# A decoder layer on one NeuronCore: pair b reordered and partly premade, three pairs by seven products in the first down linear, eight block sums made every seven chunks

## The chip, the cores and the metric

The kernel runs on one core of one Trainium2 chip. The metric is the device time of one execution in microseconds (us). Five engines work side by side, each with its own instruction stream in a fixed order: TensorE (PE in the profile, its weight loads PEld), VectorE (DVE), ScalarE (ACT), GpSimd (POOL) and SyncE (SP). SP and POOL issue the transfers (DMAs) between main memory (HBM) and on-chip memory (SBUF). TensorE writes its sums into eight PSUM banks.

## The reference, cut to what matters

One hybrid decoder layer in float32 on 272 tokens (16 learned meta tokens and 256 real ones), width 2048, feed-forward width 5632:

```python
h = rms_norm(s, norm_ffn1);  s = s + 0.5 * swiglu_ffn(h, ffn1_w_gu, ffn1_w_down)
h = rms_norm(s, norm_mix)
q, k, v, b_gate, c_gate, u = split(h @ w_in)
y_att  = diff_attention(q, k, v, lam, subln)          # 8 heads, causal, a = p0 - lam * p1
y_conv = b_gate * short_conv(c_gate * u, conv_w)      # 3 taps
gates = sigmoid(h @ w_gate)                           # two branches
merged = gates0 * (y_att @ w_branch0) + gates1 * (y_conv @ w_branch1)
s = s + merged @ w_out
h = rms_norm(s, norm_ffn2);  s = s + 0.5 * swiglu_ffn(h, ffn2_w_gu, ffn2_w_down)
return rms_norm(s, norm_final)[:, 16:]
```

Nearly all of the time is in the matrix products with the large weights.

## The kernel before, in words

**Float32 by three products.** Every float32 operand is split in two parts, high and low: weights into tiles `wh` (a cast on ScalarE) and `wl` (the rest, a subtraction on VectorE), activations likewise. A product is three matmuls: high by `wh`, low by `wh`, high by `wl`. So each weight tile costs TensorE its matmuls, ScalarE one cast and VectorE one subtraction; a tile of 128x1024 weights is loaded by SP into a buffer `st` (three buffers), and `wh` and `wl` have four buffers each.

**Stages.** In order: the first feed-forward (lines `pg`, `pu`, `pd`), then `k` (first half), `q`, `b`, `v` (first half), `k`, `v` (second halves), `c`, `u`, `c`, `u`, then four times gates `g` and branch product `z`, then `w_out`, then the second feed-forward in three parts, each of some gate-and-up units followed by two down linears (`pd`), one for each half of the output columns ("long" down linears in the first two parts, 16 chunks each).

**Seven products instead of eight.** The functions `linear` and `linear_tok` do plain products. `linear_mix` treats its input in pairs of chunks as a 2x2 by 2x2 block product. A plan gives a kind to each pair: "D" does the eight block products (24 matmuls of 128x512), "S" and "P" do seven products (21 matmuls) on sums of weight blocks and sums of activation blocks. For S the sums of the weight blocks (tiles `t13` and `t24`) are made by VectorE in place, three additions over 128x2048 elements in all; for P they were made earlier in the program, stored to HBM in a tensor `made`, and are loaded by two SP transfers of 512 KB beside a shorter weight load. A plan has four parts: the kinds by position, the positions after which transposes that have been put off (`later`) are done, where the sums of a later S are made, and the order of the pairs (empty: 0 to 7). `t13` and `t24` come from a pool `tt` of two buffers. In a D pair four PSUM banks are in use; once an S or P pair has begun, all eight are, until the products end.

**Making the sums ahead.** An object of class `Making` makes half of one pair's sums: `fetch` loads four weight blocks (512 KB, tile `mk`) by a POOL transfer, `add` does three VectorE additions, `store` writes the result (512 KB) by a POOL transfer. Steps are hung on `tick`, which `linear` calls once per chunk of the plain linears. Ticks 0 to 511 are the first feed-forward and make 54 pairs, with three fetches ahead. Ticks 528 to 639 are the seven linears from `v` to `u` (16 ticks each). There `tick_later` makes the pairs in `MADE_LATER`, one after the other: at a step it emits the add and the store of the last fetched half and then the next fetch, into one of the two `tt` buffers in turn. POOL issues these in order, so a fetch goes out behind the store before it, and a store behind its add. An add stands in VectorE's stream and waits there for its fetch; whatever VectorE has behind it waits too.

**What stands around the attention.** From the second `k` on, work of the attention is put between chunks: `scores` of one unit (matmuls `sc_ps`, then on VectorE lines 960 to 975 with exponentials on ScalarE between), and in the next step `turn` (TensorE transposes `aT`, which read `sc`) and `values`. The order of each engine's instructions is fixed at build time by a scheduler that merges these streams.

## Time and profile before

| | |
|---|---|
| median of 3 runs | 2124.77 us (2124.61 to 2125.13) |
| the profiled execution's own time | 2126.45 us |
| its span, first to last instruction | 2124.7 us |
| TensorE matmul busy | 2112.8 us, 13087 matmuls |
| VectorE busy | 1780.5 us |
| ScalarE busy | 1151.1 us |
| granted TensorE clock | 0.999 |
| stretch of b | 856.6 to 900.0 us |
| stretch of v to u | 900.0 to 1092.5 us |
| first gates unit g | 1092.5 to 1133.3 us |
| first long down linear, first half of the columns | 1600.8 to 1643.2 us |

The profile is of one execution, whose own time is 1.68 us above the median. Times inside it are counted from its first instruction. A row of the timeline gives start, duration, engine, line, operation, what is written and read, and in brackets the engine's idle time before it and what ended that. Line numbers are those of the kernel before; in the changed kernel they are one to three higher in the parts spoken of.

### The profile page before, as it was taken

The numbers are of one execution on the slowest core, as the hardware profiler recorded it, in microseconds if no ns is written. First come the engines' busy times: TensorE is split into PE (matmuls) and PEld (weight loads), VectorE is DVE, ScalarE is ACT, GpSimd is POOL, SyncE is SP. The second block draws the span as 40 slices with busy tenths as digits, with TensorE's granted clock in tenths as the row PEclk, the third lists the DMA queues.
The fourth block names the chain that finished last, engine by engine and source line by source line (L and its number), as shares of the span: only waits on it lengthen the run. The fifth ranks groups of instructions, "written<-read, shape, count | busy, mean of one in ns | idle before, by whom it ended". The sixth has DMA issues, their size and how long they took to land. (4 is left out here: it accounts for less than half of the span.)

```text
span 2124.7 us, 33643 instructions
## 1 busy us (share of the span) xinstructions
PE 2112.8 (99%) x13087; PEld 1910.3 (90%) x13087; DVE 1780.5 (84%) x2490; ACT 1151.1 (54%) x1453; POOL 164.6 (8%) x261
## 2 busy tenths in 40 slices
PE   9999999999999999999999999999999999999998
PEld 9999999999999998899998888887888888888887
DVE  8777776677777778978888899999999899998998
ACT  6434443344443445655456565567775567656765
POOL 0111111111121110000000000000000100000000
PEclk9999999999999999999999999999999999999999
DMA  7989999999889785565565665567885988779963
GB/s 303 338 316 331 344 338 327 334 325 335 332 326 340 296 301 196 202 227 199 209 220 201 233 213 190 201 225 242 314 298 194 287 316 302 261 228 314 325 236 139
DMA packets 111328, 576.47 MB, mean 271 GB/s; under 512 B 12992, under 2 KB 13376, under 8 KB 71104
## 3 DMA queue, kind: packets, MB, share of 16 engines
q1 hardware_dynamic: 74160, 444.66, 58.4%
q0 software_dynamic: 36576, 128.99, 17.4%
q8 instruction: 102, 1.67, 0.3%
q10 hardware_dynamic: 432, 0.67, 0.1%
q14 instruction: 58, 0.48, 0.1%
HBM read 506.11 MB, written 63.96 MB: 268 GB/s over the span
## 5 line engine op out<-in xcount | busy, mean ns | idle before, releaser
L429 ACT CAST wh<-st 128x1024 fp32r<-128x1024 f32 x320 | 335.2, 1049 | 471.3 <-PE pu L446 145.7
L434 DVE TENSOR_TENSOR wl<-st,wh 128x1024 fp32r<-128x1024 f32 x320 | 390.5, 1223 | 211.4 <-ACT wh L429 211.2
L552 DVE TENSOR_TENSOR wl<-st,wh 128x1024 fp32r<-128x1024 f32 (+1 forms) x424 | 453.5, 1085 | 44.4 <-ACT wh L551 40.1
L551 ACT CAST wh<-st 128x1024 fp32r<-128x1024 f32 (+1 forms) x424 | 386.6, 942 | 172.4 <-PE pdx L665 43.2
L551 ACT CAST wh<-t 128x1024 fp32r<-128x1024 f32 x214 | 224.6, 1053 | 201.9 <-DVE t L707 83.9
L552 DVE TENSOR_TENSOR wl<-t,wh 128x1024 fp32r<-128x1024 f32 x214 | 257.9, 1221 | 29.9 <-ACT wh L551 26.0
L447 PE MATMUL pd<-mh,wl 128*128 128x272 f32 x704 | 203.1, 288 | 0.0
L445 PE MATMUL pg<-h,wh 128*128 128x272 f32 x704 | 201.8, 287 | 1.0 <-ACT wh L429 1.0
L445 PE MATMUL pd<-mh,wh 128*128 128x272 f32 x704 | 202.2, 287 | 0.0
L445 PE MATMUL pu<-h,wh 128*128 128x272 f32 x704 | 201.9, 287 | 0.0
L447 PE MATMUL pu<-h,wl 128*128 128x272 f32 x704 | 201.7, 287 | 0.0
L446 PE MATMUL pu<-h,wh 128*128 128x272 f32 x704 | 201.7, 287 | 0.0
L446 PE MATMUL pg<-h,wh 128*128 128x272 f32 x704 | 201.6, 287 | 0.0
L447 PE MATMUL pg<-h,wl 128*128 128x272 f32 x704 | 201.1, 287 | 0.1
L446 PE MATMUL pd<-ml,wh 128*128 128x272 f32 x704 | 200.8, 285 | 0.0
L664 PE MATMUL pg<-wh,h 128*128 128x512 f32 x375 | 146.4, 390 | 0.3 <-ACT wh L551 0.3
L665 PE MATMUL pg<-wh,h 128*128 128x512 f32 x375 | 146.7, 391 | 0.0
L666 PE MATMUL pg<-wl,h 128*128 128x512 f32 x375 | 146.0, 389 | 0.0
L339 POOL DMA_DIRECT2D made<-mk x118 | 86.1, 729 | 760.0 <-DVE mk L333 608.4
L445 PEld LDWEIGHTS pg<-h,wh 128*128 128x128 f32 x704 | 132.6, 188 | 1.2 <-ACT wh L429 1.2
L446 PEld LDWEIGHTS pd<-ml,wh 128*128 128x128 f32 x704 | 133.5, 190 | 0.0
L447 PEld LDWEIGHTS pg<-h,wl 128*128 128x128 f32 x704 | 132.1, 188 | 0.6 <-DVE wl L434 0.5
(392 smaller groups left out, 5100.7 us busy)
## 6 DMA issues: line engine op xcount, KB each, us to landing
st<-in_ffn_w_gu_dram SPq DMA_DIRECT2D x118, 1024.0 KB, 7.5
st<-in_ffn_w_down_dram SPq DMA_DIRECT2D x82, 1024.0 KB, 7.3
mk<-in_ffn_made_of_dram POOLq DMA_DIRECT2D x118, 512.0 KB, 8.5
made<-mk POOLq DMA_DIRECT2D x118, 512.0 KB, 6.6
t<-made SPq DMA_DIRECT2D x118, 512.0 KB, 5.9
st<-in_ffn_w_gu_dram SPq DMA_DIRECT2D x54, 768.0 KB, 6.0
st<-in_w_in_dram SPq DMA_DIRECT2D x32, 1024.0 KB, 5.4
st<-in_w_gate_dram SPq DMA_DIRECT2D x27, 1024.0 KB, 4.8
```

What stands on the lines that cost most here:

```text
L339: last_store[:] = [nc.gpsimd.dma_start(out=self.unit[self.p][:, :, cs], in_=self.t).ins]
L429: nc.scalar.copy(out=wh[:, :m, :], in_=sw)
L434: last_wl[:] = [nc.vector.tensor_sub(wl[:, :m, :], sw, wh[:, :m, :].bitcast(F32)).ins]
L445: nc.tensor.matmul(a, wh[:, i, f], act.part(c, 0, t0, t1), start=first, stop=False)
L446: nc.tensor.matmul(a, wh[:, i, f], act.part(c, 1, t0, t1), start=False, stop=False)
L447: nc.tensor.matmul(a, wl[:, i, f], act.part(c, 0, t0, t1), start=False, stop=last)
L551: part_last[:] = [nc.scalar.copy(out=wh, in_=src).ins]
L552: part_last.append(nc.vector.tensor_sub(wl, src, wh.bitcast(F32)).ins)
L664: nc.tensor.matmul(ps[k], hi, wh, start=first, stop=False)
L665: nc.tensor.matmul(ps[k], lo, wh, start=False, stop=False)
L666: nc.tensor.matmul(ps[k], hi, wl, start=False, stop=left[k] == 0)
```

## The change

The diff, cut to its core:

```diff
-B_PLAN = ("DSDSDSDS", (2, 4), {(0, 1): 1, (2, 1): 3, (4, 1): 5, (6, 1): 7}, ())
+B_PLAN = ("DDSDSDPS", (1, 1), {(1, 1): 2, (3, 1): 4, (6, 3): 7}, (0, 2, 1, 4, 3, 6, 7, 5))
...
+DOWN_MADE = ("DDDPDSDP", (1,), {(4, 1): 5}, (0, 1, 3, 4, 5, 6, 7, 2))
...
-MADE = [(0, d, p) for d, plan in enumerate(GATE_UNITS) for p, kind in enumerate(plan[0]) if kind == "P"]
+MADE = [(3, 1, 7)]
+MADE += [(0, d, p) for d, plan in enumerate(GATE_UNITS) for p, kind in enumerate(plan[0]) if kind == "P"]
...
-MADE_LATER = [(0, 0, 1), (0, 0, 3), (1, 1, 5), (1, 2, 1), (1, 3, 1)]
+MADE_LATER = [(0, 0, 1), (0, 0, 3), (1, 1, 5), (1, 2, 1), (1, 3, 1), (2, 0, 4), (2, 0, 2), MADE[-1]]
...
-LATER_TICKS = (TICK_COUNT + 16, TICK_COUNT + 124)
+LATER_TICKS = [TICK_COUNT + 16 + 7 * i for i in range(2 * len(MADE_LATER))] + [TICK_COUNT + 127]
...
     def tick_later(n):
-        n0, n1 = LATER_TICKS
-        steps = len(spare_later) + 1
-        i = (n - n0) * steps // (n1 - n0)
-        if not n0 <= n < n1 or (n > n0 and i == (n - 1 - n0) * steps // (n1 - n0)):
+        if n not in LATER_TICKS:
             return
+        i = LATER_TICKS.index(n)
...
-            if p in turn_at and later:
-                later.pop(0)()
+            for _ in range(turn_at.count(p)):
+                if later:
+                    later.pop(0)()
...
-            mixed(B_PLAN, hm, w_qb[1], "b", b_end)
+            mixed(B_PLAN, hm, w_qb[1], "b", b_end, made[3][1], True)
...
-                side.extend([lambda: None] * 2)
-                side.extend(lambda p=p: ma.sum_of_parts(p) for p in (4, 6))
-                side.extend((lambda: None, lambda ma=ma: ma.sum_of_parts(2)))
-                add_mix(DOWN_FIRST, ma, w_down, half[0] * GC, u, 0.5, "dma", lambda: None)
+                for p in (None, 4, None, 6, 2) if half is thirds[0] else (None, None, 4, 6, None, 2):
+                    side.append((lambda: None) if p is None else lambda ma=ma, p=p: ma.sum_of_parts(p))
+                if half is thirds[0]:
+                    add_mix(DOWN_MADE, ma, w_down, 0, u, 0.5, "dma", lambda: None, made[2][u])
+                else:
+                    add_mix(DOWN_FIRST, ma, w_down, half[0] * GC, u, 0.5, "dma", lambda: None)
```

In b the pairs 1, 3, 5 and 7 are done by seven products, as before, but two D pairs come first, pair 7 is of kind P with sums made in the first feed-forward, and all four put-off transposes of q come after position 1. In the first long down linear (first half of the columns) pairs 4, 6 and 2 are done by seven products, 4 and 2 of them premade; before, pairs 4 and 6 were. `MADE_LATER` has eight pairs, 16 halves, with a step every seven ticks from tick 528 and a last one at tick 639, the last chunk of u; before it had five pairs, ten halves, at 11 steps over 108 ticks.

Three places show how the instructions move. First, TensorE in b. `qb_ps` are the put-off transposes of q (from `cgate` and `cup`), `bx` and the other `b_` are b's eight products, `h_` and `sp_` the activations. Before, near the end of b:

```order
L664 MATMUL b_9799<-wh,h_123 128x512
L889 MATMUL qb_ps<-ident,cgate 128x128 x8
L665 MATMUL b_9799<-wh,h_123 128x512
L889 MATMUL qb_ps<-ident,cup 128x128 x8
L666 MATMUL b_9799<-wl,h_123 128x512
```

In the changed kernel, inside the second D pair (those from `cup` stand in the same way twelve matmuls later, behind it):

```order
L664 MATMUL bx<-wh,h_118 128x512
L665 MATMUL bx<-wh,h_118 128x512
L666 MATMUL bx<-wl,h_118 128x512
L890 MATMUL qb_ps<-ident,cgate 128x128 x8
L664 MATMUL b_9795<-wh,h_118 128x512
L665 MATMUL b_9795<-wh,h_118 128x512
L666 MATMUL b_9795<-wl,h_118 128x512
```

The transposes have moved from the last pair of b, where they stand between the three matmuls of one product, to the ends of two D tiles early in b.

Second, VectorE in the attention, in the first u linear, at the softmax of one unit (`rs`, `sc` and `scM`). Before, this stands there:

```order
L434 TENSOR_TENSOR wl<-st,wh 128x1024
L971 RECIPROCAL rs<-sm 128x2
L972 TENSOR_TENSOR rs<-rs,lam 128x1
L973 TENSOR_SCALAR sc<-sc,rs 128x272
L975 SCALAR_TENSOR_TENSOR sc<-sc,rs 128x256
L975 SCALAR_TENSOR_TENSOR scM_9120<-sc,rs 128x16
```

Now:

```order
L434 TENSOR_TENSOR wl<-st,wh 128x1024
L972 RECIPROCAL rs<-sm 128x2
L973 TENSOR_TENSOR rs<-rs,lam 128x1
L333 TENSOR_TENSOR mk<-mk 128x512
L974 TENSOR_SCALAR sc<-sc,rs 128x272
L334 TENSOR_TENSOR mk<-mk 128x256
L976 SCALAR_TENSOR_TENSOR sc<-sc,rs 128x256
L976 SCALAR_TENSOR_TENSOR scM_9120<-sc,rs 128x16
L335 TENSOR_TENSOR mk<-mk 128x256
```

The three additions of a making now stand inside the chain that writes `sc`. The making before it keeps its place.

Third, SP around the start of the gates unit g. `t_` are the tiles `t24` (first of each two) and `t13` of a P pair. Before:

```order
L416 DMA st<-in_w_in_dram 128x2048 x27
L693 DMA t_12539<-made_10330 128x1024
L416 DMA st<-in_w_in_dram 128x2048
L694 DMA t_12538<-made_10330 128x1024
L686 DMA st<-in_w_gate_dram 128x2048
L686 DMA st<-in_w_gate_dram 128x1536
```

Now:

```order
L416 DMA st<-in_w_in_dram 128x2048 x28
L687 DMA st<-in_w_gate_dram 128x2048
L687 DMA st<-in_w_gate_dram 128x1536
L687 DMA st<-in_w_gate_dram 128x2048
L694 DMA t_12577<-made_10277 128x1024
L687 DMA st<-in_w_gate_dram 128x1536
L695 DMA t_12576<-made_10277 128x1024
```

The loads of the first P pair's sums, which reuse the two buffers of the last two makings, have moved behind the first three and four weight loads of g.

More of the change, by code (lines that the diff above doesn't have):

```diff
@@ L312, in drain @@
             ahead.pop(0)[0]()
-    made = [[{} for _ in range(n)] for n in (D // GW, F // GW, 2)]
+    made = [[{} for _ in range(n)] for n in (D // GW, F // GW, 2, 2)]
     class Making:
@@ L840, in after1 @@
             side.extend((norm2.end, norm2.end_tok))
-        if c % 2 and c > 3 and B_PLAN[0][c // 2] == "S":
+        if c % 2 and c > 3 and Q[0][c // 2] == "S":
             side.append(lambda p=c // 2: hm.sum(p))
@@ L1200, in turned, with add_mix @@
             )
-    def add_mix(plan, a, w, k0, u, by, adds, end):
+    def add_mix(plan, a, w, k0, u, by, adds, end, made=None):
         v = [[sT[i][u][:, q * GW : (q + 1) * GW] for q in range(2)] for i in range(2)]
@@ L1252, in done @@
                 pending.append(finish_adds)
-        linear_mix(plan, a, w[u], "pd", done, k0)
+        linear_mix(plan, a, w[u], "pd", done, k0, made, True)
     def out_done(u):
@@ L1427, in _laid_out @@
     d["ffn2_w_gu"] = np.stack([_in_pairs(np, a["ffn2_w_gu"][0], c, F + c) for c in range(0, F, GW)])
-    ws = [(a["w_gate"][0], D, GW), (a["ffn2_w_gu"][0], F, GW), (a["w_out"][0], GW, W2)]
+    ws = [(a["w_gate"][0], D, GW), (a["ffn2_w_gu"][0], F, GW), (a["ffn2_w_down"][0], GW, W2), (a["w_in"][0], GW, 3 * W2)]
     d["ffn2_made_of"] = np.stack(
```

## The prediction

> **What bounds the kernel now.** First the page, then TensorE's waits over the whole span:
>
> ```profile
> PE 2112.8 (99%) x13087; PEld 1910.3 (90%) x13087; DVE 1780.5 (84%) x2490; ACT 1151.1 (54%) x1453; POOL 164.6 (8%) x261
> PE warm L105 <- DVE ones L99: 1.1, 1, 1.1
> PE pg L445 <- ACT wh L429: 1.0, 1, 1.0
> PE pg L664 <- ACT sp L634: 0.7, 1, 0.7
> PE pg L664 <- ACT wh L551: 0.3, 1, 0.3
> PE u L447 <- DVE wl L434: 0.3, 1, 0.3
> PE qb_ps L889 <- ACT u2x L749: 0.2, 1, 0.2
> ```
>
> TensorE is busy nearly throughout; the columns of the waits are the total in us, the number and the longest, and they sum to 3.6 us. So there are two ways to gain: fewer matmuls, or the last two waits, which lie in u and in b. And there is one way to lose: to make something late that is in time today. For that I read the windows of b and of v to u (us of the window, then busy us and instructions of PE, PEld, DVE, ACT, POOL), and what VectorE waits for from 895 to 1094:
>
> ```profile
> 857.00:899.00 42.00, 41.80 (x192) 34.14 (x191) 38.90 (x45) 24.36 (x30) 0.56 (x1) 1.00 0.60 208
> 900.00:1093.00 193.00, 192.69 (x1550) 184.31 (x1549) 157.99 (x343) 98.33 (x192) 12.06 (x19) 1.00 0.61 213
> DVE wl L434 <- ACT wh L429: 21.3, 17, 2.4
> ```
>
> From v to u VectorE has 35 us free of 193, and most of its waiting is for ScalarE's casts, which wait for a free buffer: it is ahead there. Six more additions of halves fit in as an amount; the question is where each stands.
>
> **Three matmuls fewer.** In the long down linear one D pair (24 matmuls) becomes a P pair (21). The price of one comes from q, whose plan has 4 x 24 + 4 x 21 = 180 of this shape:
>
> ```profile
> 815.83:856.63 40.80, 40.80 (x183) 1.00 0.54 187
> ```
>
> 40.80 / 180 = 0.227 us (the window counts three neighbours), so 3 x 0.227 = 0.68 us go. VectorE makes one set of sums there instead of two. Its tiles for a P are four instead of two, which the three D pairs ahead of it cover (3 x 24 x 0.227 = 16 us); without that cover one cast and one subtraction, 1.05 and 1.22 us by the rows of their kind below, would be late. I take **-0.7 us**.
>
> **b.** TensorE's rows around the put-off transposes:
>
> ```profile
> 894.16 0.39 PE L664 MATMUL b<-wh,h 128*128 128x512 f32 x1
> 894.74 1.06 PE L889 MATMUL qb_ps<-ident,cgate 128*128 128x128 f32 x8 [0.19 <-ACT u2x L749]
> 895.56 0.48 PE L665 MATMUL b<-wh,h 128*128 128x512 f32 x1
> 896.05 1.14 PE L889 MATMUL qb_ps<-ident,cup 128*128 128x128 f32 x8
> 896.94 0.48 PE L666 MATMUL b<-wl,h 128*128 128x512 f32 x1
> 897.26 0.39 PE L664 MATMUL b<-wh,sp 128*128 128x512 f32 x1
> ```
>
> A matmul should hold the next up by 0.227; here the next comes after 0.58, 0.49 and 0.32, which is 0.35 + 0.26 + 0.09 = 0.70 us lost. The transposes need PSUM banks, and with S second in b all eight are taken until `bx` has been copied out (`u2x`). Two D pairs first leave four banks free, so they can run early. They themselves (0.82 and 0.89 us for eight) stay. Pair 7 as P takes one set of sums, 1.22 + 0.68 + 0.68 us by VectorE's rows of those shapes, off VectorE; two more loads on SP stand ahead of v's, whose buffers are filled well ahead. Bounds: -0.7 if nothing waits at the new place, and +1.1, one late cast, if the last S, whose sums must wait until the P before it gives up the two `tt` buffers, comes late. I take **-0.7**: VectorE's load in b falls.
>
> **The making, seven chunks apart.** A fetch goes out behind the store before it, so from one add to the next there pass an add, the issue of the store and a landing. The transfers from 890 to 1100 (median us to landing), and the least, median and most of fetches and stores together from 890 to 1100:
>
> ```profile
> mk<-in_ffn_made_of_dram POOLq DMA_DIRECT2D x10, 512.0 KB, 6.1
> made<-mk POOLq DMA_DIRECT2D x10, 512.0 KB, 4.2
> t<-made SPq DMA_DIRECT2D x4, 512.0 KB, 4.0
> DMA to landing us min/median/max: 3.1/5.2/9.9
> 1066.91 0.69 DVE L331 TENSOR_TENSOR mk<-mk 128x512 f32<-128x512 f32 x1 [2.11 <-DMA mk<-in_ffn_made_of_dram]
> 1067.63 0.43 DVE L332 TENSOR_TENSOR mk<-mk 128x256 f32<-128x256 f32 x1
> 1068.09 0.43 DVE L333 TENSOR_TENSOR mk<-mk 128x256 f32<-128x256 f32 x1
> ```
>
> That is 1.6 + 0.7 + 6.1 = 8.4 us, up to 12.2 with the longest landing. The distance was 108 / 11 = 9.8 chunks and becomes 7; a chunk takes 193 / 112 = 1.72 us, so 16.9 us become 12.0. On average that suffices, but an add stands where the scheduler put it, and the wait for a fetch stops all of VectorE behind it. Where VectorE is ahead of TensorE by more than the wait, nothing comes of it. I see three places where it is not.
>
> *An attention unit in u.* The order shows an add inside the chain that writes `sc`, behind the same earlier add as before, whose store and fetch are these (with the landings of the transfers issued from 1023 to 1024.5):
>
> ```profile
> 1022.78 0.71 POOL L339 DMA_DIRECT2D made<-mk  x1 [25.26 <-DVE rs L972]
> 1023.43 0.61 POOL L327 DMA_DIRECT2D mk<-in_ffn_made_of_dram  x1
> st<-in_w_in_dram SPq DMA_DIRECT2D x1, 1024.0 KB, 7.8
> mk<-in_ffn_made_of_dram POOLq DMA_DIRECT2D x1, 512.0 KB, 7.8
> 1028.03 0.16 DVE L972 TENSOR_TENSOR rs<-rs,lam 128x1 f32<-128x1 f32 x1
> 1028.22 0.36 DVE L973 TENSOR_SCALAR sc<-sc,rs 128x272 f32<-128x272 f32 x1
> 1028.62 0.48 DVE L975 SCALAR_TENSOR_TENSOR sc<-sc,rs 128x256 f32<-128x256 f32 x1
> 1030.56 0.38 PE L984 MATMUL aT<-ident,sc 128*128 128x128 f32 x2
> ```
>
> The fetch landed at 1023.4 + 7.8 = 1031.2. The add will now be reached at 1028.2, so VectorE stands still for 3.0 us; then 0.69 + 0.36 + 0.43 + 0.48 = 2.0 us, and `sc` is ready at 1033.2 where `aT` wants it at 1030.56: TensorE waits 2.6 us. With the median landing of 6.1 it is 0.9, with 3.1 nothing, with 9.9 4.7. I take **+2.6**, since the fetch and its neighbour, a 1 MB load, are the same.
>
> The Trainium skill, page "DMA: Bandwidth & Descriptors", section "Anatomy of one DMA — SWDGE (gpsimd) path", gives a transfer issued from GpSimd 2.0 us and its bytes over 436 GB/s, for 512 KB an estimate of 3.2 us. By it no add here would wait, and the sum would be that of the first rival; the trace has 7.8 for this very transfer and 6.1 as the median, and the measurement decides.
>
> *The second u.* The add at 1066.91 made the block behind it late (the wait `u L447` above). TensorE comes later now by what the attention costs, so this wait goes: **-0.3**; if the fetch lands 3.8 us later than the median it is +3.
>
> *The first gates unit.* The load of `t13` takes the buffer of the last making. Now that stands at tick 639, before at 627. The last store before, the load behind it, and the users:
>
> ```profile
> 1068.92 0.71 POOL L339 DMA_DIRECT2D made<-mk  x1 [11.38 <-DVE rsao L285]
> 1073.65 0.33 SPq L694 DMA_DIRECT2D t<-made  x1
> 1095.28 1.05 ACT L551 CAST wh<-t 128x1024 fp32r<-128x1024 f32 x1 [1.56 <-PE gx L665]
> 1096.52 1.22 DVE L552 TENSOR_TENSOR wl<-t,wh 128x1024 fp32r<-128x1024 f32 x1
> 1099.71 1.22 DVE L552 TENSOR_TENSOR wl<-st,wh 128x1024 fp32r<-128x1024 f32 x1
> 1103.19 0.39 PE L666 MATMUL g<-wl,h 128*128 128x512 f32 x1
> ```
>
> Twelve chunks later is 1068.9 + 12 x 1.72 = 1089.6 for the last store, if its add finds its fetch landed. It stands six chunks (10.3 us) behind the one before, whose three parts have two or three other VectorE operations between them (some 3 us), so it misses a median fetch: I put the store at 1092.5. Then 4.2 for the store and 4.0 for the load: `t13` lands at 1100.7, say 1101, where its cast began at 1095.28 before. Behind it on ScalarE and VectorE stand the next pair's tiles: the second subtraction ended at 1100.93, 5.65 us after the cast began, so now at 1106.65; TensorE wants it at 1103.19, plus the 2.3 us by which it is late already: it waits 1.2 more. Without the earlier lateness it would be 3.5. With the shortest fetch (3.1) the store is at 1089.6, `t13` lands at 1097.8, and 0.3 remain; with the longest (9.9) `t13` lands at 1104.5 and 4.7 are added. I take **+1.2**.
>
> **The sum**, against the profiled execution's own 2126.45: -0.7 - 0.7 + 2.6 - 0.3 + 1.2 = +2.1, 2128.55. That execution lies 1.68 above the median of the runs, so the forecast is **2126.9 us**. A measurement of this kernel can hardly tell less than 0.2% (4.25 us) from no change; this is inside it.
>
> **Rivals.** *All landings in time.* Fetches of 3 to 5 us, as the 3.1 of the range shows that there are, and a scheduler's order that fits: then only the gains stand, -1.4 (the wait in u stays), **2123.4**. For it: VectorE's 35 free us and but one wait for a fetch before. Against it: that one wait came with 16.9 us between steps on average. Chance 0.27.
>
> *`t13` late by much (the slow side).* Place: the first P pair of g; price: every us by which `t13` lands behind 1097.5 (1103.19 - 5.65) is a us of TensorE. It decides the sign beyond what can be told once the sum passes +4.25, that is, `t13` lands at 1103.2 or later (5.65 - 1.4). With a last fetch of 9.9 us, the store at 1096.3 and 4.2 + 4.0 behind it, `t13` lands at 1104.5: +7.0 - 1.4 = +5.6, **2130.4**. For it: the fetch that kept VectorE until 1066.91 was a late one, in just this stretch. Against it: 9.9 is the longest of the view. Chance 0.19, with the attention's 4.7 counted here.
>
> *b gains nothing.* The early transposes wait for q's results, or the last S for its sums: -0.7 is lost, and the rest as forecast, 2127.6. Chance 0.06; it lies inside the forecast's own range.
>
> *The change doesn't do what it says*: the order shows three matmuls fewer and the transposes early, so only the waits are open. No chance of its own.
>
> **How the numbers follow.** Forecast 0.48, the first rival 0.27, the slow one 0.19, b 0.06. The forecast's own range is 2124.5 to 2129 (landings of 5 to 8 us). The range for 8 in 10 reaches down to the first rival, 2123.3, and up to the slow one, 2130.2. Faster by over 0.2% would need 4.25 us, and the gains are 1.7 with the wait in u: 0.02. Slower by over 0.2%: the slow rival, 0.19. The rest, 0.79, is no change that can be told.
>
> **What would show it.** Right: no `qb_ps` wait near the end of b and b shorter by 0.7; the down linear at 41.7 us instead of 42.4; `mk` landings as a wait of VectorE in several places; TensorE's waits with `aT` on `sc` in u, and with g on the first P pair's tiles. Wrong: no wait of TensorE between 1020 and 1110, with fetches of 4 us (the first rival); a wait in g of more than 5 us (the second); or a wait in b or in the down linear, where I see none. What would overturn the argument is a TensorE wait for an early part of the making, from v to the first c, where I count VectorE as far enough ahead.

## The result and the profile after

| | before | changed |
|---|---|---|
| median, runs side by side | 2124.95 us | 2137.29 us (2135.89 to 2139.79) |
| ratio, 95% interval | | 1.0059 (1.0046 to 1.0072) |
| profiled execution, its span | 2126.45, 2124.7 | 2136.65, 2134.9 |

The change costs 12.3 us, 0.59%. The forecast was 2126.9 with a range up to 2130.2: the sign of the small loss came out as forecast, the size did not, and the time lies above the range. Ranges and ratios, here and below, leave out single executions at a granted clock of 0.752 or less (2613 us and more); the others lie at 0.986 to 0.999.

Line numbers are now those of the changed kernel: `L333` to `L335` are the three additions of a making, `L976` writes `sc` and `scM`; the lines of the weights (`L434`, `L552`, `L664` to `L666`) are numbered as before.

The engines' busy time and the longest waits of TensorE in the changed kernel (total us, number, longest):

```profile
PE 2115.2 (99%) x13084; PEld 1911.7 (90%) x13084; DVE 1785.5 (84%) x2504; ACT 1152.7 (54%) x1455; POOL 172.1 (8%) x273
PE aT L985 <- DVE scM L976: 4.7, 2, 2.3
PE g L666 <- DVE wl L552: 1.7, 2, 1.2
PE pa L922 <- DVE vz L921: 0.9, 1, 0.9
PE g L664 <- ACT wh L551: 0.9, 1, 0.9
PE gx L664 <- DVE yf L1044: 0.7, 1, 0.7
PE u L447 <- DVE wl L434: 0.6, 1, 0.6
```

The three matmuls are gone (13087 to 13084) and so is the wait in b, but there is a row for `aT` with 4.7 us in two places, and one of these was not forecast.

Where the time went is read from the windows of the stages. The columns are the stretch, its length, then busy time and instructions of PE, PEld, DVE, ACT, POOL, the granted clock, the DMA share and GB/s. First the changed kernel: b, the second `k`, the first `u`, the second `u`, the first gates unit, the first long down linear (both halves of the columns):

```profile
855.99:898.58 42.59, 42.59 (x198) 35.44 (x196) 37.66 (x43) 26.09 (x31) 0.00 (x0) 1.00 0.61 216
...
924.06:956.86 32.80, 29.51 (x233) 27.62 (x232) 24.68 (x61) 14.70 (x27) 3.78 (x6) 1.00 0.67 249
...
1016.49:1048.72 32.23, 29.91 (x233) 28.20 (x232) 26.55 (x66) 14.86 (x34) 2.53 (x4) 0.95 0.54 195
...
1073.28:1099.36 26.08, 25.39 (x210) 24.80 (x209) 21.78 (x49) 10.32 (x13) 2.52 (x4) 1.00 0.71 251
1099.36:1144.99 45.63, 42.30 (x182) 33.48 (x181) 42.28 (x57) 25.48 (x30) 0.71 (x1) 1.00 0.68 241
1611.24:1695.15 83.91, 83.91 (x375) 69.46 (x374) 77.67 (x98) 48.02 (x55) 3.55 (x4) 1.00 0.73 247
```

The same stretches of the kernel before:

```profile
856.63:899.98 43.35, 43.15 (x197) 35.26 (x196) 40.23 (x46) 25.32 (x30) 0.56 (x1) 1.00 0.59 206
...
925.50:954.66 29.16, 29.16 (x232) 27.57 (x231) 23.08 (x58) 14.76 (x27) 2.53 (x4) 1.00 0.62 224
...
1014.30:1042.74 28.44, 28.44 (x233) 26.90 (x232) 26.68 (x67) 14.86 (x34) 2.53 (x4) 1.00 0.65 220
...
1067.31:1092.54 25.23, 24.92 (x211) 24.71 (x210) 24.31 (x51) 10.99 (x13) 0.71 (x1) 1.00 0.61 215
1092.54:1133.34 40.80, 40.80 (x182) 33.80 (x181) 37.00 (x49) 24.33 (x28) 0.00 (x0) 1.00 0.65 228
1600.75:1685.34 84.59, 84.59 (x379) 70.00 (x378) 78.10 (x99) 46.40 (x53) 3.58 (x4) 1.00 0.72 237
```

So b gains 0.76 and the down linear 0.68, as forecast. The losses are 3.64 us in the second `k` (not forecast), 3.79 in `u`, 0.85 in the second `u` and 4.83 in the first gates unit: 13.1 us, of which 11.7 remain after the gains. The stages between are as they were. The two profiled executions lie only 10.2 us apart; the 1.5 us in between are at the start and in the second feed-forward, where the kernel did not change (the first `pg` stretch alone is 25.5 to 28.0 us long in the profiles of this case).

What holds TensorE up is shown by the chain of work that ended last, in order of time (start, us, what). Among its longest pieces are five fetches:

```profile
932.87 8.10 DMA mk<-in_ffn_made_of_dram
...
1025.62 7.69 DMA mk<-in_ffn_made_of_dram
...
1056.90 7.31 DMA mk<-in_ffn_made_of_dram
...
1067.90 5.82 DMA mk<-in_ffn_made_of_dram
...
1091.30 7.41 DMA mk<-in_ffn_made_of_dram
```

A background transfer has come onto the path that sets the end. VectorE's timeline in the second `k` shows how:

```profile
928.70 0.69 DVE L333 TENSOR_TENSOR mk<-mk 128x512 f32<-128x512 f32 x1 [3.28 <-DMA mk<-in_ffn_made_of_dram]
929.30 0.70 DVE L921 COPY vz<-vt 128x16 f32<-128x16 f32 x8
...
931.39 0.41 DVE L335 TENSOR_TENSOR mk<-mk 128x256 f32<-128x256 f32 x1
...
941.06 0.69 DVE L333 TENSOR_TENSOR mk<-mk 128x512 f32<-128x512 f32 x1 [2.66 <-DMA mk<-in_ffn_made_of_dram]
...
943.31 0.35 DVE L976 SCALAR_TENSOR_TENSOR sc<-sc,rs 128x128 f32<-128x128 f32 x1
943.58 0.23 DVE L976 SCALAR_TENSOR_TENSOR scM<-sc,rs 128x16 f32<-128x16 f32 x1
```

and TensorE's the consequence:

```profile
929.61 0.79 PE L922 MATMUL pa<-ident,vz 128*128 128x128 f32 x4 [0.94 <-DVE vz L921]
943.81 0.30 PE L985 MATMUL aT<-ident,sc 128*128 128x128 f32 x1 [2.35 <-DVE scM L976]
```

VectorE stands before an addition until the fetch has landed. Behind it in its order stand the copies into `vz`, and the second time the chain that writes `sc`; TensorE waits for both; it has no wait for `wl`, the weights' part, here.

In `u`, VectorE and then TensorE:

```profile
1033.40 0.69 DVE L333 TENSOR_TENSOR mk<-mk 128x512 f32<-128x512 f32 x1 [3.02 <-DMA mk<-in_ffn_made_of_dram]
...
1035.01 0.23 DVE L976 SCALAR_TENSOR_TENSOR scM<-sc,rs 128x16 f32<-128x16 f32 x1
```

```profile
1035.23 0.66 PE L985 MATMUL aT<-ident,sc 128*128 128x128 f32 x2 [2.32 <-DVE scM L976]
```

This is the wait that was forecast, and nearly in its size. But 2.3 us do not make 3.8. The rest is the granted clock, the third column from the end; first a piece just behind the wait in the second `k`, then one just behind the wait in `u`:

```profile
943.80:946.00 2.20, 2.19 (x18) 2.20 (x19) 2.20 (x5) 0.71 (x2) 0.54 (x1) 1.00 0.67 246
1035.20:1038.00 2.80, 2.77 (x13) 2.80 (x14) 2.62 (x7) 0.38 (x1) 1.27 (x2) 0.50 0.29 97
```

After its wait of 2.32 us TensorE ran at half its clock for 2.8 us, which costs another 1.4 us; after the 2.35 us in the second `k` it did not.

In the first gates unit the last addition is late first (VectorE's timeline):

```profile
1098.80 0.69 DVE L333 TENSOR_TENSOR mk<-mk 128x512 f32<-128x512 f32 x1 [3.63 <-DMA mk<-in_ffn_made_of_dram]
```

then the load of `t13`, which goes out when the last store has landed (SP's timeline, then that load in the view of transfers: KB, us from issue to landing),

```profile
1104.62 0.33 SPq L695 DMA_DIRECT2D t<-made  x1
```

```profile
t<-made SPq DMA_DIRECT2D x1, 512.0 KB, 4.5
```

the cast that needs it on ScalarE,

```profile
1109.17 1.04 ACT L551 CAST wh<-t 128x1024 fp32r<-128x1024 f32 x1 [4.40 <-PE g L665]
```

and TensorE's waits for both:

```profile
1102.26 0.50 PE L664 MATMUL gx<-wh,h 128*128 128x512 f32 x1 [0.65 <-DVE yf L1044]
...
1110.27 0.50 PE L664 MATMUL g<-wh,sp 128*128 128x512 f32 x1 [0.89 <-ACT wh L551]
```

`yf` is late by the wait at 1098.80; `t13` lands at 1104.62 + 4.5 = 1109.1, the cast follows at once, and three waits of TensorE follow it. (The cast's row names TensorE as what released it, whose matmul ended in the same tenth of a microsecond; in the second profile of this kernel the row names the load.)

### The profile page after: what moved, and what is told of

The parts are those of the page before. It is cut to its first block, busy times and chain, and to the rows that moved or that the text cites. A ratio compares the mean times of both kernels' runs of the same rounds, so it can differ in the third digit from the quotient of the medians.

```text
span 2134.9 us, 33699 instructions
## 1 busy us (share of the span) xinstructions
PE 2115.2 (99%) x13084; PEld 1911.7 (90%) x13084; DVE 1785.5 (84%) x2504; ACT 1152.7 (54%) x1455; POOL 172.1 (8%) x273
## 4 chain that ended last, share of the span: by engine, by line
PE 51%; DVE 2%; DMA 2%; issue 0%; ACT 0%; POOL 0%; DVEq 0%; ACTq 0%
PE pg L664 6%; PE pg L666 6%; PE pg L665 6%; PE pd L664 4%; PE pd L665 4%; PE pd L666 4%; PE g L666 2%; PE g L664 2%; PE g L665 2%; DMA mk<-in_ffn_made_of_dram 2%; PE z L479 1%; PE z L481 1%; PE z L480 1%; PE pdx L664 1%; PE pdx L665 1%; PE pdx L666 1%
## 5 line engine op out<-in xcount | busy, mean ns | idle before, releaser
L434 DVE TENSOR_TENSOR wl<-st,wh 128x1024 fp32r<-128x1024 f32 x320 | 390.3, 1222 | 203.1 <-ACT wh L429 202.7
L552 DVE TENSOR_TENSOR wl<-st,wh 128x1024 fp32r<-128x1024 f32 (+1 forms) x424 | 452.8, 1082 | 45.6 <-ACT wh L551 41.3
L552 DVE TENSOR_TENSOR wl<-t,wh 128x1024 fp32r<-128x1024 f32 x216 | 260.1, 1220 | 31.2 <-ACT wh L551 27.3
L664 PE MATMUL pg<-wh,h 128*128 128x512 f32 x375 | 146.3, 390 | 0.0
L666 PE MATMUL pg<-wl,h 128*128 128x512 f32 x375 | 146.0, 389 | 0.0
L445 PEld LDWEIGHTS pg<-h,wh 128*128 128x128 f32 x704 | 133.0, 189 | 0.4 <-ACT wh L429 0.4
L446 PEld LDWEIGHTS pg<-h,wh 128*128 128x128 f32 x704 | 133.0, 189 | 0.0
```

The source lines that it names most:

```text
L434: last_wl[:] = [nc.vector.tensor_sub(wl[:, :m, :], sw, wh[:, :m, :].bitcast(F32)).ins]
L445: nc.tensor.matmul(a, wh[:, i, f], act.part(c, 0, t0, t1), start=first, stop=False)
L446: nc.tensor.matmul(a, wh[:, i, f], act.part(c, 1, t0, t1), start=False, stop=False)
L552: part_last.append(nc.vector.tensor_sub(wl, src, wh.bitcast(F32)).ins)
L664: nc.tensor.matmul(ps[k], hi, wh, start=first, stop=False)
L666: nc.tensor.matmul(ps[k], hi, wl, start=False, stop=left[k] == 0)
```

## The experiments

Theory A: VectorE takes its instructions in order and stands before an addition until the fetch has landed; the distance between the steps decides. Theory B: it is the amount of additions, theory C the amount of transfers. All stage lengths are collected in a table at the end of this section.

**The same work, no wait for a landing.** Of the changed kernel:

```diff
 in tick_later, at step i:
-    spare_later[i - 1].add()
+    # three additions of a constant into the next buffer, ahead of its fetch
+    nc.vector.tensor_add(v[:, 0:4, :], const, const)
+    nc.vector.tensor_add(v[:, 4:6, :], v[:, 0:2, :], const)
+    nc.vector.tensor_add(v[:, 6:8, :], v[:, 4:6, :], const)
     spare_later[i - 1].store()
     spare_later[i].fetch(...)
```

> The changed kernel, but the three VectorE additions of each later making no longer read what was fetched: they add a constant (the identity matrix) into the buffer ahead of the fetch, so VectorE does the same amount of work at the same ticks and never waits for a landing; the fetch then overwrites the buffer and it is stored unsummed (the sums of the eight later pairs are left out, so the output is not the reference's). Theory A (VectorE takes its instructions in order and stands before an addition until the fetch has landed; the attention chain behind it is late): the waits in the second k (+3.6 us in the changed kernel), in the first half of u (+3.8) and in the second u (+0.9) go, the last load in the first gates unit stays late: 2137.3 - 8.3 = about 2129, between 2126 and 2130. Theory B (it is the amount: six more halves of VectorE additions and of transfers): 2135 to 2138, as in the changed kernel.

Measured: 2125.21 us (2124.14 to 2125.81), ratio to before 0.9999 (0.9990 to 1.0009). The second `k`, `u` and the second `u` are at 29.12, 28.44 and 24.65 us, without a wait; the gates unit keeps 0.8 of its 4.8. Theories B and C fall: VectorE's additions, the fetches and the stores are as many and as large. (Some rows around the additions lie in another order too, so the next experiment is the cleaner one.) It came out a little below what theory A gave, because the load in the gates unit is earlier too: `t13` lands 5.7 us after the unit's first matmul instead of 9.7. VectorE waits once, 2.7 us, for a store to land.

**The fetch ahead of the addition.** Of the changed kernel:

```diff
 in tick_later, at step i:
-    if i: spare_later[i - 1].add(); spare_later[i - 1].store()
     if i < len(spare_later): spare_later[i].fetch(N_AUX + i % 2, i < 2)
+    if i: spare_later[i - 1].add(); spare_later[i - 1].store()
```

> The changed kernel with one order turned round: in each step the fetch of the next half is issued ahead of the addition and the store of the last one, so that it waits only for the buffer (the store one step earlier) and no longer for VectorE. The additions stay on VectorE at their places. Theory A: a fetch goes out some 5 us earlier or more, the 20 us for which VectorE waits for landings fall below 5, and the second k, u and the second u are nearly as before the change: 2124 to 2129, depending on what the last load in the first gates unit still costs. Theory B (amount) and theory C (traffic): 2135 to 2138.

Measured: 2124.07 us (2122.98 to 2127.56), ratio to before 0.9997 (0.9988 to 1.0005). The additions keep their places to within three rows of VectorE; in `u` they begin two rows earlier, still ahead of the operations that write `sc`. VectorE's wait for `mk`, in the changed kernel from 890 to 1115 this row (total us, number, longest), is not in its list any more:

```profile
DVE mk L333 <- DMA mk<-in_ffn_made_of_dram: 20.1, 7, 4.1
```

The second `k` and both `u` are free of waits. The profiled execution is the slowest of eleven; the window of its gates unit still has a wait:

```profile
1090.13:1134.51 44.38, 41.96 (x182) 33.56 (x181) 37.10 (x50) 24.02 (x28) 0.00 (x0) 1.00 0.66 228
```

**And six chunks apart.** The kernel of the last experiment with one number changed, so that the last addition stands at tick 624 instead of 639 (before: 627):

```diff
-LATER_TICKS = [TICK_COUNT + 16 + 7 * i for i in range(2 * len(MADE_LATER))] + [TICK_COUNT + 127]
+LATER_TICKS = [TICK_COUNT + 16 + 6 * i for i in range(2 * len(MADE_LATER) + 1)]
```

> The changed kernel with the fetch issued ahead of the addition (as in the run where the fetch goes first) and the steps six chunks apart instead of seven, so that the last addition stands at tick 624, three chunks ahead of before's 627, instead of 639. Theory A': with the fetch first no wait for a landing comes back at six chunks, and the 3.5 us that the first gates unit waited for its load of made sums in that run's profile go: 2122.5 to 2124, that is 2125.0 less 1.4 and less the 0.6 in the second u. If the load was late for another reason than the last making's place: 2124 to 2127, with the wait in the first gates unit as before. If six chunks are too close: waits for landings as in the changed kernel, 2128 or more.

Measured: 2123.70 us (2123.23 to 2124.96) beside 2125.28 for the kernel before, ratio 0.9994 (0.9985 to 1.0003). The gates unit's window no longer has one:

```profile
1091.15:1131.99 40.84, 40.84 (x183) 33.80 (x181) 36.97 (x49) 24.33 (x28) 0.00 (x0) 1.00 0.63 224
```

So its loss came from the place of the last making. No stage in the table below is longer than before by more than 0.04 us; the medians differ by 1.6 us, which is too little to tell from no change.

**The additions on GpSimd.** Of the changed kernel, twice: first only the engine of the later additions, then also the loads of made sums held behind the weight load of their own pair in the issue order.

```diff
-    nc.vector.tensor_add(v[:, 0:2, :], v[:, 0:2, :], v[:, 1:3, :])
+    nc.gpsimd.tensor_add(v[:, 0:2, :], v[:, 0:2, :], v[:, 1:3, :])
 (and the other two)
...
 in load(p), the second time only:
+    with tc.issue_after(own):    # own: the load of st
         nc.sync.dma_start(out=t24s[p], in_=made[pairs[p]][:, 2:4, :])
         nc.sync.dma_start(out=t13s[p], in_=made[pairs[p]][:, 0:2, :])
```

> The changed kernel with the three additions of each later making done by GpSimd instead of VectorE, so that the wait for a landing stands on GpSimd, which has nothing else to do here. Theory A: the second k, u and the second u are as before the change; the gain of 1.4 us (b and down linear) comes out, and what is left is the last load in the first gates unit, +1 to +5: 2124.5 to 2128.5; if the makings are done earlier this way, as little as 2123.5. Theory B (VectorE's amount): also about 2124 to 2128. Theory C (the transfers themselves, by the traffic they add): 2134 to 2138.

> The additions of the later makings on GpSimd, as before, but each load of made sums on SyncE is now held behind the load of its own pair's weights in the issue order; in the earlier run with GpSimd the first gates unit's load of made sums stood ahead of three weight loads of u and kept them back until the last making was stored (a wait of 54 us). Theory A': without that the second k, u, the second u and the first gates unit wait less than 1 us each: 2123 to 2125. If GpSimd's additions slow VectorE or the loads down: 2126 or more.

Measured: 2181.63 us the first time, a miss by every theory, and 2125.50 (2124.81 to 2127.82) the second, 1.0003 (0.9995 to 1.0012). The first has one wait of TensorE of 54 us, in `u`. It comes from SP and ends with ScalarE's cast, behind which `aB` stands (TensorE's row, SP's, then ScalarE's):

```profile
1077.65 2.54 PE L959 MATMUL sc_ps<-kT,qT 64*128 64x272 f32 x4 [54.00 <-ACT aB L990]
```

```profile
1069.21 0.33 SPq L696 DMA_DIRECT2D t<-made  x1
1069.62 1.56 SPq L417 DMA_DIRECT2D st<-in_w_in_dram  x3
```

```profile
1076.28 1.04 ACT L430 CAST wh<-st 128x1024 fp32r<-128x1024 f32 x1 [60.42 <-DMA st<-in_w_in_dram]
```

With the additions on GpSimd the scheduler put the gates unit's loads of `t24` and `t13` ahead of three weight loads of `u` on SP; they waited for the last store, and SP's queue with them. Held in place, the gates unit is free again and the second `k` loses 1.2 us, which is told below. So moving the wait to an engine that nobody waits for takes the loss away too, though the time lies between the two figures of the expectation and shows no gain.

**The changed kernel again.**

> The changed kernel once more, unaltered, beside the runs below and with a second profile. Theory A' (VectorE waits in order for landings; once an addition has had to wait, the next fetch, which goes out behind it, is late too): median 2135 to 2139 as before, scattered by some 3 us from run to run, and the profile again with waits of TensorE in the second k, in u and in the first gates unit. If only the first profile was unlucky: below 2130.

Measured: 2138.32 us (2136.03 to 2143.86), ratio 1.0065 (1.0051 to 1.0078). The profile has the waits at the same places (`aT` in the second `k` and in `u`, the second `u`, four in the gates unit); only that for `vz` is not there, and the stretch at half the clock follows the wait in the second `k` (2.45 us) instead of that in `u` (2.06). The loss is a property of the kernel.

**Each part alone.** The kernel before with the down linear's part only (seven pairs, seven chunks apart, ticks 528 to 626; b and its sums as before), and with b's part only (six pairs, 8.25 chunks apart, ticks 528 to 627):

```diff
 down linear alone
-B_PLAN = ("DDSDSDPS", ...)          +B_PLAN = ("DSDSDSDS", ...)
-MADE = [(3, 1, 7)]; MADE_LATER = [..., (2, 0, 4), (2, 0, 2), MADE[-1]]
+MADE_LATER = [..., (2, 0, 4), (2, 0, 2)]
 b alone
-MADE_LATER = [..., (2, 0, 4), (2, 0, 2), MADE[-1]]
+MADE_LATER = [..., MADE[-1]]
+LATER_TICKS = [TICK_COUNT + 16 + 99 * i // 12 for i in range(13)]
```

> The kernel before with only the down linear's part of the change: seven pairs (two of them for the down linear) made seven chunks apart, at ticks 528 to 626; b as before. The last addition stands where it did before the change (627). b +0, down linear -0.7. Theory A': the second k has a wait in some executions only, as with the five pairs seven apart (0 to 3.6); u has additions again and waits about 3.8; the first gates unit does not wait, since the last making is no later than before: 2125.0 - 0.7 + 3.8 = 2128, up to 2132. Theory D (what stalls is started by b's new order, which lets VectorE arrive earlier): 2124 to 2125.

> The kernel before with only b's part: b in the new order with its last pair made early, hence six pairs made later, 8.25 chunks apart, ticks 528 to 627. b -0.76, down linear as before. Theory A': at 8.25 chunks (14.2 us) the additions find their fetches landed, mostly: 2125.0 - 0.8 = 2124.2, up to 2126 with one wait of 1 to 2 us. Theory D: the waits in the second k and u are there although the distance is larger: 2129 or more.

Measured: the down linear alone 2128.80 us (2128.09 to 2133.03), 1.0020 (1.0010 to 1.0029); b alone 2124.59 (2123.86 to 2125.37), 0.9996 (0.9988 to 1.0005). The first loses in `u` (30.68) and the second `u` (26.27), not in the second `k` (29.14) nor in the gates unit (40.84): with the last addition no later than before, that stall does not arise. The second gains b's 0.76, and at 8.25 chunks the waits are small (29.35 and 29.06 us in the second `k` and in `u`). Theory D falls as it was put: with more distance the new b does no harm.

**The distance alone.** Before's five pairs seven chunks apart; b's part alone with seven instead of 8.25; and the changed kernel with the old b:

```diff
 five pairs:  LATER_TICKS of before  ->  [TICK_COUNT + 16 + 7 * i for i in range(11)]
 b alone:     99 * i // 12           ->  7 * i
 old b:       B_PLAN, its made pair and MADE as before, MADE_LATER with eight pairs
```

> The kernel before with one thing changed: its five pairs are made seven chunks apart (ticks 528 to 598) instead of 9.8 apart. The amount of additions and transfers is that of before. Theory A: the two waits in the second k come back, since the additions there stand at the same places as in the changed kernel (+3.6), and the waits in u and the second u don't, since no addition is left there: about 2128.5, between 2127 and 2130. Theory B (the amount): 2125, as before.

> b's part alone, as in the run of b alone, but its six pairs are made seven chunks apart (ticks 528 to 612) instead of 8.25. One number differs. Theory A' (distance): the second k waits as in the changed kernel (about 2.8 to 3.6) and u too (2.3 to 3.8), no wait in the second u and in the first gates unit, since no making is left there: 2124.6 + 5 to 7 = 2130 to 2132. If the distance is harmless without the two pairs of the down linear (amount): 2124 to 2125.

> The changed kernel with b put back: the down linear's part and eight pairs made seven chunks apart up to tick 639, b in its old order and 0.76 longer. Theory D' (b's new order makes VectorE reach the additions of the second k earlier and puts v's loads beside the fetches): no wait in the second k, as in the runs with the old b; u +2.3, second u +1.0 and first gates unit +4.7 as in the changed kernel: 2125.0 - 0.7 + 2.3 + 1.0 - 0.6 + 4.7 = 2131.7, between 2130.5 and 2133. If the second k does not depend on b: 2134.5 to 2137.

Measured: five pairs 2125.14 us (2123.98 to 2128.57), 1.0003 (0.9994 to 1.0013), where 2128.5 was expected; b alone at seven 2132.47 (2131.73 to 2135.50), 1.0040 (1.0025 to 1.0055); the old b with eight pairs 2135.20 (2133.26 to 2139.76), 1.0052 (1.0038 to 1.0066). That median lies in the range of the other theory, a second `k` that does not depend on b, but the profile (of an execution of 2136.83) has no wait there: it is `u` that loses 4.4 instead of 2.3, since behind its wait of 2.66 us the granted clock was 0.68 from 1037 to 1040. What the other executions had is not shown. For b alone, 8.25 to 7 chunks is one number and costs 7.9 us, so the distance it is. But the second `k` waits only where b has its new order: 32.80 and 33.52 us in the two profiles of the change and 34.10 here, against 29.12 to 29.14 in the three profiles with the old b at seven chunks. The five pairs' miss belongs here: six of its ten runs lie at 2124.0 to 2125.5 and four at 2126.1 to 2128.6, so a wait of this size may come with the old b too, in some executions; the profile is of one of the six, and no run shows it.

**What b has to do with it.** Two more. In the first the down linear's part alone, its very first fetch two ticks later, as late after the start of `v` as with the new b. In the second b alone at seven chunks, its first addition moved up by one row on VectorE:

```diff
 late first fetch:      +LATER_TICKS[0] = TICK_COUNT + 18     (was 16)
 early first addition:  +LATER_TICKS[1] = TICK_COUNT + 21     (was 23)
```

> The run with the down linear's part alone (seven pairs, seven chunks apart, b in its old order, 2128.8 us), but the very first fetch goes out two ticks later, so that it leaves at about the start of v, as it does with b's new order (0.1 to 0.9 us after the start of v there, 3.6 us ahead of it with the old one). On VectorE one 60 ns memset moves three rows, everything else stands as it stood. Theory E (b's new order frees the two buffers later, and the late first fetch, beside a 1 MB load, passes its delay on from step to step): the wait in the second k is there, +2.8 to +5: 2131.5 to 2134. Theory F (the late first fetch is harmless; the second k waits with the new b because VectorE's work at the end of b and v's loads lie otherwise): 2128 to 2130, no wait in the second k.

> The run with b's part alone and six pairs made seven chunks apart (2132.5 us, with waits in the second k and in u), but the first addition one step earlier on VectorE: its rows stand ahead of one more weight subtraction (1.2 us) than there, all other rows as they stood. The store and the second fetch so leave about 1.1 us earlier, at 10.7 us after the start of v instead of 11.9, as in the runs with the old b (10.6). Theory G (a delay of a microsecond at the first step is passed from fetch to addition to fetch and grows to the wait in the second k; with the old b the chain starts that microsecond earlier): the second k's wait falls from 5 us to below 1.5, u's stays: 2128 to 2129.5. Theory H (the fetches land later with the new b for another reason, such as the loads that lie beside them): 2131 to 2133, the second k as it was.

Measured: the late first fetch 2130.40 us (2127.40 to 2135.92), 1.0031 (1.0020 to 1.0041), between the two theories; its profile is the fastest of its nine runs and has no wait in the second `k`, so it can't say what the slower ones had. The early first addition 2128.14 (2126.66 to 2129.65), 1.0013 (1.0003 to 1.0023): theory G. The window of the second `k`, first without and then with the one row moved:

```profile
924.48:958.58 34.10, 31.08 (x232) 29.18 (x231) 24.77 (x61) 14.67 (x27) 3.78 (x6) 0.95 0.65 235
```

```profile
924.54:953.67 29.13, 29.13 (x233) 27.54 (x231) 24.53 (x61) 14.80 (x27) 3.78 (x6) 1.00 0.73 254
```

and GpSimd's second fetch in the timeline of each (`v` starts at 899.00 and 899.06):

```profile
910.86 0.62 POOL L329 DMA_DIRECT2D mk<-in_ffn_made_of_dram  x1
```

```profile
909.32 0.62 POOL L329 DMA_DIRECT2D mk<-in_ffn_made_of_dram  x1
```

Worked out from such rows, the start of the second, third and fourth fetch in us after the start of `v`, for all profiles at seven chunks in which a fetch goes out behind a store:

```
                          2nd    3rd    4th    second k
changed                  11.15  21.99  34.29    32.80
changed, again           11.46  21.49  33.32    33.52
b alone, seven           11.86  21.74  33.80    34.10
down linear alone        10.63  20.64  31.70    29.14
five pairs, seven        10.63  20.47  30.86    29.12
old b, eight pairs       10.69  20.20  31.21    29.14
late first fetch         10.64  20.53  30.90    29.14
b alone, one row moved   10.26  20.05  30.86    29.13
```

Half a microsecond to 1.6 at the second fetch has become 1.6 to 3.4 at the fourth, whose landing the score chain of the second `k` needs. A late landing makes the addition late, the addition the store, the store the next fetch. What this does not settle is why the landings are longer in the late ones too (7.6 to 8.0 us for the third fetch against 5.7 to 6.8): the loads beside it lie a little differently, and no run separates that.

The stages of all kernels (length in us by their profiles, from the first matmul of one stage to that of the next) and the medians:

```
                            b    second k     u    second u    g     median
before                    43.35   29.16    28.44   25.23   40.80   2124.95
changed                   42.59   32.80    32.23   26.08   45.63   2137.29
changed, again            42.59   33.52    30.74   25.82   45.52   2138.32
same work, no wait        42.59   29.12    28.44   24.65   41.64   2125.21
fetch ahead               42.59   29.12    28.44   24.65   44.38   2124.07
fetch ahead, six chunks   42.59   29.14    28.44   24.65   40.84   2123.70
additions on GpSimd       42.59   29.92    86.93   24.65   40.84   2181.63
  and loads held          42.59   30.36    28.44   24.65   40.84   2125.50
down linear alone         43.35   29.14    30.68   26.27   40.84   2128.80
  late first fetch        43.40   29.14    30.69   25.66   40.80   2130.40
b alone, 8.25 chunks      42.59   29.35    29.06   24.63   40.80   2124.59
b alone, seven            42.59   34.10    31.78   24.65   40.84   2132.47
  one row moved           42.59   29.13    32.98   24.65   40.84   2128.14
five pairs, seven         43.38   29.12    28.44   24.65   40.84   2125.14
old b, eight pairs        43.35   29.14    32.85   26.22   45.26   2135.20
```

## Why the prediction was wrong

**The two gains: right.** Down linear -0.7 forecast, 0.68 measured. b -0.7 forecast, 0.76 in every profile with the new b, 0.69 as a difference of medians in the run of b alone. There was no late cast.

**"On average that suffices ... I see three places where it is not": wrong, and the largest miss.** The second `k` was priced at nothing and costs 3.6. The step that failed is the one that set 8.4 us of need against 12.0 us between steps. The 8.4 counted one addition as 1.6 us and its store as 0.7; but an addition's three parts stand apart on VectorE, with weight subtractions between them, and it has waited itself. In the changed profile the third fetch left at 920.57, and VectorE reached the addition for it at 928.70 - 3.28 = 925.4, the fourth at 932.87 and 941.06 - 2.66 = 938.4: 4.9 and 5.5 us were left for a landing of 8. The need was 12.3 us, not 8.4: 8.1 from the third fetch to its landing, 3.1 until the last of the three parts had ended (931.80), 1.1 until the next fetch went out at 932.87; and that is more than the 12.0 between steps. Nor does "VectorE ahead of TensorE" by its weights help: the additions stand ahead of `vz` and `sc`. By the rows above VectorE's waits of 3.28, 2.66 and 3.02 us became waits of TensorE of 0.94, 2.35 and 2.32, so that VectorE was only 2.3, 0.3 and 0.7 us ahead there. The closing sentence of the prediction named this place as what would overturn it.

**u, +2.6: mechanism and wait right, size off.** VectorE's wait was put at 3.0 us and was 3.02, that of TensorE at 2.6 and was 2.32. The stage lost 3.8, since the granted clock was 0.50 for the next 2.8 us. In the other profiles where `u` waits for a fetch (b alone at 8.25 chunks aside) the stage loses 2.2 to 2.3 us where the clock stays full and 3.3 to 4.5 where it does not. The step that failed here is the price of a wait, which was its length alone: that it can be followed by a stretch at half the clock was not in the sum.

**The second u, -0.3: wrong sign.** It lost 0.85. The argument was that TensorE comes later by what the attention costs and so finds the block ready. It does not hold, since the fetch came later still. Before, it went out 10.4 us ahead of the stage's first matmul (1056.93 against 1067.31) and had landed 0.4 us ahead of it; now it went out only 5.4 us ahead (1067.90 against 1073.28) and landed 0.4 us behind it, although its 5.82 us are less than the 6.9 of the median here.

**The gates unit, +1.2: place and cause right, size off by 3.6.** The load was put 8.5 us after the unit's start (1101 against 1092.5) and landed 9.7 after (1109.1 against 1099.4). The step that failed is "plus the 2.3 us by which it is late already": the same error as in the second `u`, since the last addition, its store and the load were late as well. Without this credit the prediction had 3.5, and the load's landing 1.2 us later makes it 4.7 of the 4.83. The wait for `yf` was not seen, but adds nothing: what TensorE loses there it does not wait for `t13`'s tiles later, and the kernel with the fetch ahead, which has no such wait, fits the following as well. The price of the slow rival, a microsecond for each one by which `t13` lands late, is borne out: in five profiles (changed, again, old b with eight pairs, fetch ahead, no wait for a landing) it lands 9.7, 9.6, 9.3, 8.5 and 5.7 us after the unit's first matmul, and the unit loses 4.8, 4.7, 4.5, 3.6 and 0.8. The runs with the last addition at 624 to 627 have none of this loss.

**The rivals.** The slow one had the right place for a third of the loss. That of all landings in time describes the kernel with the fetch ahead: 2123.4 was its figure, 2123.7 and 2124.1 were measured there. Its reason, fetches of 3 to 5 us, was misread: the 3.1 of the view is that of a store. Of the ten fetches before, the shortest took 3.8 us and the other nine 5.1 to 9.9, and in the changed kernel the median was 6.9; with the fetch ahead they still took 5.2 in the median, but went out earlier.

**The range** held every landing known before, but each stall by itself: it took the fetches as independent, where one late landing makes the next fetch late.

## What to carry to other kernels

A wait for a transfer on an engine that works in order costs everything queued behind it, so compare the landing with the time from the issue to the place where the consumer stands, not with the average distance, and put the next fetch ahead of the work on the last one. A stall that moves TensorE also moves whatever keeps step with it, so it earns no credit at the next place. Before a background job is made denser, look which chains its steps stand in, and what the last step still holds.

## What was not expected of the hardware

**The clock after a short wait.** Beside the 0.50 above, b alone at seven chunks had half the clock twice, behind its wait of 2.58 us in the second `k` and behind this one in `u` (TensorE's row, then the window):

```profile
1036.26 0.41 PE L985 MATMUL aT<-ident,sc 128*128 128x128 f32 x2 [1.62 <-DVE scM L976]
```

```profile
1037.13:1040.55 3.42, 3.42 (x19) 3.42 (x18) 2.59 (x6) 1.85 (x5) 1.13 (x2) 0.50 0.68 192
```

Half of 3.42 us is 1.7 us, as much again as the wait; the stage lost 3.34. By the Trainium skill, page "TensorE: Matmul & The Clock Gate", section "Why this matters for your kernels", gaps of more than about 3 us between bursts bring half the clock. That half the clock follows a wait agrees; the length does not. In the profiles of this case waits of 1.62, 2.32, 2.45, 2.58, 2.66 and 2.79 us were followed by it, and waits of 2.00, 2.01, 2.06 and 2.35 us were not. What decides between them is not shown here.

**GpSimd beside VectorE.** With the additions on GpSimd and the loads held, one weight subtraction of VectorE and one addition of GpSimd that run at the same time:

```profile
941.14 2.33 DVE L435 TENSOR_TENSOR wl<-st,wh 128x1024 fp32r<-128x1024 f32 x1
```

```profile
942.47 1.60 POOL L335 TENSOR_TENSOR mk<-mk 128x256 f32<-128x256 f32 x1
```

The first takes 1.22 us elsewhere, the second 0.73. In the next pair only GpSimd is slower:

```profile
944.03 1.21 DVE L435 TENSOR_TENSOR wl<-st,wh 128x1024 fp32r<-128x1024 f32 x1
```

```profile
944.15 1.68 POOL L336 TENSOR_TENSOR mk<-mk 128x256 f32<-128x256 f32 x1
```

The 2.33 us stand ahead of `sc` in VectorE's order, and TensorE then waits 1.05 us for it, which is most of what that kernel lost in the second `k`. The page "GPSIMD Engine Reference" of the Trainium skill, section "8. Key points", says that GpSimd shares its SBUF interfaces with VectorE and contends with VectorE instructions that have two SBUF inputs; these rows agree.
